# Measured durations in a generator that orders a decoder step for five engines

## The chip, the cores and the metric

The kernel runs on one core of a Trainium2 chip. The metric is the device time of one execution in microseconds (us); lower is better. Five engines each work through a list of instructions of their own, in order: TensorE (PE), VectorE (DVE), ScalarE (ACT), GpSimd (POOL) and SyncE (SP), which issues nearly all transfers. They wait for each other through semaphores only.

## The reference

One layer of a decoder, for 512 prompt tokens and for 8 sequences of 4 new tokens, each of which has 4096 tokens of past in a paged cache. In short:

```python
glu_a, glu_b, q, k, v, g_conv, g_att = split(x @ w_in)          # d_model 1024
u = glu_a * sigmoid(glu_b)
conv_out = silu(layer_norm(causal_depthwise_conv(u))) @ w_conv_proj
z = q @ k_all.T / 8 + sb_bias                                    # 8 heads of 64, keys: past pages + new
log_1m = log_sigmoid(-z) where the mask allows, else 0
a = exp(log_sigmoid(z) + cumsum_from_the_right(log_1m) - log_1m) # stick-breaking attention
att_out = (a @ v_all) @ w_att_proj
mixed = (sigmoid(g_conv) * conv_out + sigmoid(g_att) * att_out) @ w_out
x = layer_norm(alpha * x + mixed)
y = layer_norm(alpha * x + swiglu(x) + sigmoid(x @ w_ple_gate) * (p @ w_ple))
```

Everything is float32. The cache holds 8 x 32 pages of keys and as many of values that this step reads, 512 pages of 256 KB each, 134 MB in all.

## The kernel before, in words

**Products.** The prompt and the 32 new tokens stand side by side as 544 columns. A product of the main line (tile `g`) multiplies 128 x 128 of a weight with 272 columns (256 or 288 in some stages, 512 for q, k and the attention projection). Weights and activations are split in a high and a low half (`wh`, `wl`; `xh`, `xl`), and each product is made in three passes (`passes`). A weight comes in units of 512 KB: a raw tile (`wr`, three buffers, or `wq` and `wa` in the big pool), which ACT or DVE copies to `wh` and DVE or POOL subtracts from to get `wl`. A raw tile is free again when its second `wl` is done.

**Decode attention.** 32 chunks, each of 2 pages of keys for 4 sequences (8 transfers, `kv<-in_ck`) and the 8 pages of values (`kv<-in_cvv`). A page is one transfer. For each chunk PE makes scores (`z<-kv,qblk`, 16 matmuls, 32 records in the trace), ACT and DVE make the attention weights (`dz`, `dl`, `dp`, a scan that carries `cnew` from chunk to chunk), PE transposes them (`tp<-cct,dz`) and multiplies them with the values (`av<-kv,dp`, 8 matmuls, 16 records). Page tiles come from a pool of 39 slots that other tiles use too; at most 17 hold pages at a time (a tile is two pages), fewer in some stages.

**Prompt attention and convolution.** Prompt attention (`pa_pair`: `z<-qk`, `tp<-qk`, tiles `pa` and `pb`) and the convolution on DVE (`c<-u,cvt,c`, 120 instructions of 128 x 512) run beside the first third of the main line.

**Stages of the main line.** x times w_in (`g<-xh`), attention projection (`g<-ohl`), convolution projection (`g<-sh`), w_out (`g<-m`, in two halves of the columns A and B), the first feed-forward units and the embeddings (`g<-x1h`, `g<-ph`), the rest of the feed-forward part (`g<-x1h` with 272 columns, `g<-h`) and the last norm. After the last chunk the new tokens' attention output passes through w_att_proj and w_out by twelve weight tiles (`wa`; products `z<-wa,o_s` and `z<-wa,m_s`) and a norm of its own (`sq_s`, `r_s`, `y_s`), and only then can the 272-column feed-forward products start.

**What sets the order.** The program is written by a generator at build time. `Weave` keeps a clock for PE (`t`), ACT, DVE, POOL and the transfers (`dma`), all in us of an imagined execution. Each stream of work (main line, page loads, scores, decode, prompt attention, convolution, norms) is a Python generator that yields until a tile is ready by these clocks, and the scheduler lets the first stream go on that may. `mm` and `tr` add an estimate to PE's clock, `Engine` one to the clock of ACT, DVE or POOL, `moved` one to that of the transfers. `tt` and `split` choose between DVE, POOL and ACT by which is estimated to end first. So the numbers set no time on the chip; they set in which order each engine's instructions stand, and on which engine some of them run. On the chip each list is worked through in that order, and an instruction that must wait holds up all that is behind it on its engine. This is as true of SP: `prefetch` (pages) and `loader` (weights) write into one list.

Of the kernel before, what the change touches and what calls it, by code (L numbers as in the profile page):

```python
# [56 lines left out]
class Weave:  # L57
# [10 lines left out]
    def op(self, clock, us, out, reads):  # L68

        start = max([getattr(self, clock), self.t] + [self.ready.get(a.name, 0.0) for a in reads])  # L70
        setattr(self, clock, start + us)
        self.ready[out.name] = max(self.ready.get(out.name, 0.0), start + us + LAT)

# [54 lines left out]
class Engine:  # L128
# [6 lines left out]
    def __getattr__(self, name):  # L135
        fn = getattr(self.eng, name)

        def call(**kw):
            fn(**kw)  # L139
            out = kw["out"]  # L140
            reads = [v for k, v in kw.items() if k != "out" and hasattr(v, "space")]
            n = 1
            for d in out.shape[1:]:
                n *= d
            psum = any(a.space == PSUM for a in reads + [out])
            if self.clock == "act":
                ptr = sum(hasattr(kw.get(k), "space") for k in ("scale", "bias"))
                us = (n + (61 if psum else 112) + 56 * ptr) / 1200.0
                f = kw["func"]
                if f in (AF.Exp, AF.Ln, AF.Sigmoid) and self.table != (f == AF.Sigmoid):  # L150
                    self.table = f == AF.Sigmoid
                    us += 1.3
                reads = reads[:len(reads) - ptr]
            elif self.clock == "pool":
                us = (2 * n + 100) / 960.0
            else:
                ptr = sum(hasattr(kw.get(k), "space") for k in ("scalar", "scalar1", "scalar2", "initial"))
                if name in ("tensor_scalar", "tensor_copy") and not psum:
                    n = n / 2
                us = (n + 66 + 58 * ptr) / 960.0  # L160
            self.wv.op(self.clock, us, out, reads)
            for a in reads:
                if a.space == PSUM:
                    self.wv.read[a.name] = getattr(self.wv, self.clock) + LAT
        return call
# [3 lines left out]
def step_kernel(ctx: ExitStack, tc: tile.TileContext, xT, pT, ck, cvv, state, pt, W, cv, cc, yT, kT, vT, cvo):  # L169
    nc = tc.nc  # L170
    wv = Weave()
# [42 lines left out]
    def moved(ap):  # L214
        n = 4
        for d in ap.shape:
            n *= d
        wv.dma = max(wv.dma, wv.t + 1.5) + n / 0.357e6

    def load(eng, out, in_):  # L220
        eng.dma_start(out=out, in_=in_)  # L221
# [7 lines left out]

    def mm(us, out, lhsT, rhs, start, stop):  # L230
        T.matmul(out, lhsT=lhsT, rhs=rhs, start=start, stop=stop)  # L231
        wv.t = max(wv.t, wv.ready.get(lhsT.name, 0.0), wv.ready.get(rhs.name, 0.0), wv.free.get(out.name, 0.0)) + us
        wv.ready[out.name] = wv.t + 0.2

    def tr(out, in_):
        T.transpose(out, in_, ident)  # L236
        wv.t = max(wv.t, wv.ready.get(in_.name, 0.0), wv.free.get(out.name, 0.0)) + 0.11
        wv.ready[out.name] = wv.t + 0.2

# [79 lines left out]
    anew = con.tile([128, 2, 128], F32, name="anew")  # L319
# [3 lines left out]


    raw, hl, hs_, kept = {}, {}, {}, {}
    cur = {"t": 0, "pos": 0, "next": 0, "raw": 0, "w": 0, "kv": 0}

    def held(u):

# [68 lines left out]
    def passes(p, cols, k, nk, w, x):  # L398

        wh, wl = w  # L400
        xh, xl = x
        for a, b, st, sp in ((wh, xh, k == 0, False), (wh, xl, False, False), (wl, xh, False, k == nk - 1)):
            for s, c0, c1 in cols:
                mm((c1 - c0) * 4.25e-4, p[:, s, :c1 - c0], a, b[:, c0:c1], st, sp)

    def products(p, cols, nk, rhs, base, last=True):
        for k in range(nk):
# [101 lines left out]
    qk = []  # L509
    v_sb = {}  # L510
# [41 lines left out]
    def scores():  # L552
        for c in range(NCH):
            r = c // 16
            yield lambda: (c, 0, 3) in kv_t and c - n_scan[0] < 2
            ks_ = [kv_t.pop((c, 0, j)) for j in range(4)]
            yield on(*ks_)
            yield KMARGIN
            yield wv.bank("z")
            z = bank("z")  # L560
            for m in range(4):
                for j in range(4):
                    mm(0.127, z[32 * j:32 * j + 32, :256].rearrange("p (g c) -> p g c", g=2),
                       qblk[:, 4 * r + j, m, :], ks_[j][:, :, m * 128:(m + 1) * 128], m == 0, m == 3)
            del ks_
            cur["kv"] -= 4
            zb, l = d_tiles()
            S.activation(out=zb, in_=z[:, :256], func=AF.Identity, bias=cvt[:, SBR:SBR + 1])
            chain1(zb, l)
            z_t[c] = (zb, l)  # L570
            del zb, l

    def decode():
        yield on(qblk, ks)
        for r in range(2):
            yield wv.bank("z")
            z = bank("z")
# [23 lines left out]
        for r in range(2):  # L601
            carry = cnew[:, r:r + 1]
            yield wv.bank("av")
            av = bank("av")
            for n in range(16):
                c = 16 * r + n
                yield lambda: c in z_t
                zb, l = z_t.pop(c)
                yield on(l)
                p = d_sum()  # L610
                relu(p, zb)
                scan(p, l, carry)
                minus(zb, l)
                V.tensor_copy(out=carry, in_=l[:, 0:1])
                n_scan[0] += 1
                yield on(zb)
                chain3(zb)
                yield on(zb)
                yield DMARGIN
                yield wv.bank("tp")  # L620
                tp = bank("tp")
                for g in range(2):
                    tr(tp[:, g * 128:(g + 1) * 128], zb[:, g * 128:(g + 1) * 128])
                at = p
                S.activation(out=at, in_=tp[:, :256], func=AF.Copy)
                yield on(at)
                yield DMARGIN
                yield lambda: (c, 1, 3) in kv_t
                kvs = [kv_t.pop((c, 1, j)) for j in range(4)]
                yield on(*kvs)  # L630
                for g in range(2):
                    for j in range(4):
                        mm(0.235, av[32 * j:32 * j + 32, :], at[:, g * 128 + 32 * j:g * 128 + 32 * j + 32],
                           kvs[j][:, g, :], n == 0 and g == 0, False)
                del kvs, zb, l, at, p
                cur["kv"] -= 4
                yield
            yield lambda: ("vs", r) in v_sb
            for j in range(4):
                mm(0.235, av[32 * j:32 * j + 32, :], anew[:, r, 32 * j:32 * j + 32], v_sb["vs", r], False, True)  # L640
            yield spare(1)
            ob = tmp("ob")[:, :512]
            S.activation(out=ob, in_=av, func=AF.Copy)
            yield on(ob)
            yield wv.bank("tp")
            tp = bank("tp")
            for m in range(4):
                mm(0.11, tp[:, m * 32:m * 32 + 32], ob[:, m * 128:(m + 1) * 128],
                   cct[:, SEL + m * 32:SEL + m * 32 + 32], True, True)
            drop()  # L650
            for hh in range(2):
                V.tensor_copy(out=o_s[64 * hh:64 * hh + 64, :, r, :],
                              in_=tp[64 * hh:64 * hh + 64, :128].rearrange("p (m f c) -> p m f c", m=4, f=2)[:, :, hh, :])
# [3 lines left out]
    pa = {"live": 0, "next": 0}  # L657

    def pa_pair(idx, m, tiles):
# [5 lines left out]
        seg, n = [], 0  # L665
        for i in tiles:
            w = 128 * (i + 1)
            for z, r in zip(zs, rows):
                mm(w * 1.7e-3, z[:, n:n + w], qk[m][r, 0, 128 * i:128 * i + 128], qk[m][r, 1, :w], True, True)
            seg.append((i, n, w))  # L670
            n += w
        ab = []
        yield spare(2)
        for hh, z in enumerate(zs):
            h = 2 * m + hh
            a, b = slot("pa", (128, 2, 512)), tmp("pb")
# [38 lines left out]
        for i, c, w in seg:  # L715
            for kt in range(i + 1):
                for r, (zb, l) in zip(rows, ab):
                    mm(0.125, pa["o"][r, 128 * i:128 * i + 128], v_sb[m][:, kt * 128 + r.start:kt * 128 + r.stop],
                       l[:, c + kt * 128:c + (kt + 1) * 128], kt == 0, kt == i)
        if tiles[0] == 3:  # L720
            t = slot("ohl", (128, 2, 512), dt=F32R)
# [22 lines left out]
    us, cp = {}, []  # L744
# [77 lines left out]
    def project(nk, lhs, wt, out):  # L822
        yield wv.bank("z")
        z = bank("z")
        for h in range(2):
            yield on(*[wt(4 * h + j, 0) for j in range(4)])
            for k in range(nk):
                for j in range(4):
                    mm(0.075, z[32 * j:32 * j + 32, h * 128:(h + 1) * 128], lhs(k), wt(4 * h + j, k),
                       k == 0, k == nk - 1)  # L830
                if k % 2:
                    yield
# [599 lines left out]


LAT = 0.15
VBIAS = 2.0
GBIAS = 0.3
DMA_AHEAD = 5.0
# [107 lines left out]
```

## Time and profile before

| | us |
|---|---|
| median of 3 runs (1024.55 to 1028.53) | 1025.02 |
| the profiled execution | 1026.71 |
| its span, from first to last instruction | 1024.9 |
| PE busy / DVE / ACT / POOL | 977.8 / 636.1 / 484.3 / 166.5 |
| mean granted clock of PE | 0.986 |

The profile gives, for each engine, what it did and what ended its idle time. "Busy" of PE counts the time in which at least one matmul record is open. A wait is put down to what ended it. In the tables by stage a row is: start:end, length, busy us and count of PE, PE's weight loads (PEld), DVE, ACT and POOL, then the granted clock of PE, the mean busy share of the 16 transfer engines, and the GB/s that were moved. All times in the text are of the profiled execution, counted from the start of its span; it took 1.7 us longer than the median.

### The profile page before, as it was taken

What the parts mean: (1) busy time and instruction counts of PE and PEld (TensorE: products, weight loads), DVE (VectorE), ACT (ScalarE), POOL (GpSimd) and SP (SyncE); (2) the same over time, 40 slices, a digit from 0 to 9 for tenths busy, and PEclk for the clock granted to TensorE, in tenths of its full rate; (3) what the DMA queues carried; (4) which work ended last, traced back from release to release, by engine and by line L of the source; (5) the groups of instructions that cost most, each with busy time, mean ns of one, the idle gap of its engine ahead of it and who ended that gap; (6) DMA issues with size and microseconds to landing.
All of it is one profiled execution on the core that took longest, in us unless ns stands there. A gap on an engine that the chain in (4) does not pass through costs nothing.

```text
span 1024.9 us, 22484 instructions
## 1 busy us (share of the span) xinstructions
PE 977.8 (95%) x8242; PEld 856.9 (84%) x8242; DVE 636.1 (62%) x1005; ACT 484.3 (47%) x941; POOL 166.5 (16%) x156
## 2 busy tenths in 40 slices
PE   7989999899899999999999899999999999999994
PEld 6866676677777886788777899999999999999993
DVE  4798999999756456674976654333433345323376
ACT  4635666567785974343665543233332333222224
POOL 1320423223111002233322200000000012000021
PEclk9999999999999999999999999999999999999997
DMA  9949999999889999999989352222222222222302
GB/s 355 337 161 328 326 298 353 336 311 319 283 305 315 321 345 328 360 349 327 313 295 376 105 164 82 87 99 83 84 90 96 82 83 88 98 83 82 124 1 88
DMA packets 101376, 222.00 MB, mean 217 GB/s; under 512 B 11154, under 2 KB 14483, under 8 KB 101267
## 3 DMA queue, kind: packets, MB, share of 16 engines
q1 hardware_dynamic: 99394, 217.46, 61.4%
q10 hardware_dynamic: 1872, 3.11, 0.8%
q8 instruction: 65, 1.06, 0.4%
q14 instruction: 45, 0.36, 0.1%
HBM read 215.45 MB, written 5.07 MB: 215 GB/s over the span
## 4 chain that ended last, share of the span: by engine, by line
PE 76%; DVE 10%; DMA 7%; issue 2%; SPq 2%; ACT 2%; ACTq 0%; POOL 0%; DVEq 0%; POOLq 0%
PE g L231 63%; PE z L231 6%; PE av L231 5%; DVE c L139 3%; DMA kv<-in_ck 3%; PE tp L236 1%; DMA kv<-in_cvv 1%; SPq L221 1%; PE o L231 1%; DVE pb L139 1%; DMA wr<-in_W 1%; DVE wl L139 1%; DMA wa<-in_W 1%; SPq L536 1%; DVE dl L139 1%
## 5 line engine op out<-in xcount | busy, mean ns | idle before, releaser
L139 ACT ACTIVATE wh<-wr 128x512 fp32r<-128x512 f32 x236 | 146.5, 627 | 296.3 <-PE g L231 251.4
L139 DVE TENSOR_TENSOR wl<-wr,wh 128x512 fp32r<-128x512 f32 x193 | 134.0, 700 | 167.8 <-ACT wh L139 167.0
L231 PE MATMUL g<-x1h,wh 128*128 128x272 f32 (+2 forms) x832 | 183.7, 289 | 2.2 <-ACT x1h L139 1.5
L231 PE MATMUL g<-x1h,wl 128*128 128x272 f32 (+2 forms) x832 | 182.5, 288 | 0.0
L231 PE MATMUL g<-x1l,wh 128*128 128x272 f32 (+2 forms) x832 | 182.1, 288 | 0.0
L139 POOL TENSOR_TENSOR wl<-wr,wh 128x512 fp32r<-128x512 f32 x47 | 68.4, 1458 | 535.2 <-ACT wh L139 487.9
L231 PEld LDWEIGHTS g<-x1h,wh 128*128 128x128 f32 x832 | 134.9, 188 | 4.6 <-ACT x1h L139 1.7
L231 PEld LDWEIGHTS g<-x1l,wh 128*128 128x128 f32 x832 | 134.8, 189 | 0.0
L231 PEld LDWEIGHTS g<-x1h,wl 128*128 128x128 f32 x832 | 134.0, 189 | 0.0
L231 PE MATMUL g<-xh,wh 128*128 128x272 f32 (+1 forms) x512 | 128.1, 322 | 6.0 <-ACT wh L139 6.0
L231 PE MATMUL g<-h,wh 128*128 128x272 f32 x704 | 122.3, 290 | 0.0
L231 PE MATMUL g<-xh,wl 128*128 128x272 f32 (+1 forms) x512 | 119.8, 305 | 0.2 <-POOL wl L139 0.2
L231 PE MATMUL g<-xl,wh 128*128 128x272 f32 (+1 forms) x512 | 119.8, 305 | 0.0
L139 DVE SCALAR_TENSOR_TENSOR c<-u,cvt,c 128x512 f32<-128x512 f32 x120 | 113.3, 944 | 3.3
L231 PEld LDWEIGHTS g<-xh,wh 128*128 128x128 f32 x512 | 83.7, 192 | 26.4 <-issue 16.6
L231 PEld LDWEIGHTS g<-h,wh 128*128 128x128 f32 x704 | 103.1, 189 | 0.3
L231 PEld LDWEIGHTS g<-xh,wl 128*128 128x128 f32 x512 | 83.4, 191 | 3.9 <-POOL wl L139 0.8
L231 PEld LDWEIGHTS g<-xl,wh 128*128 128x128 f32 x512 | 84.0, 192 | 2.7 <-DVE xl L139 0.5
L231 PE MATMUL g<-h,wl 128*128 128x272 f32 x352 | 80.1, 289 | 0.0
L231 PE MATMUL z<-kv,qblk 128*32 128x256 f32 x1024 | 66.2, 382 | 1.9 <-DMA kv<-in_ck 1.9
L231 PE MATMUL av<-kv,dp 128*32 128x512 f32 x512 | 63.9, 612 | 0.0
L139 ACT ACTIVATE pa<-pa 128x384 f32<-128x384 f32 (+1 forms) x96 | 52.5, 555 | 17.4 <-DVE pa L139 15.7
(222 smaller groups left out, 1401.0 us busy)
## 6 DMA issues: line engine op xcount, KB each, us to landing
kv<-in_ck SPq DMA_DIRECT2D x256, 256.0 KB, 4.2
kv<-in_cvv SPq DMA_DIRECT2D x256, 256.0 KB, 5.3
wr<-in_W SPq DMA_DIRECT2D x120, 512.0 KB, 3.6
wq<-in_W SPq DMA_DIRECT2D x15, 512.0 KB, 6.0
wa<-in_W SPq DMA_DIRECT2D x12, 512.0 KB, 9.9
xr<-in_xT SPq DMA_DIRECT2D x8, 272.0 KB, 5.6
out_yT<-pw SPq DMA_DIRECT2D x7, 272.0 KB, 2.3
out_kT<-qk ACTq DMA_DIRECT2D x4, 272.0 KB, 5.2
```

Source lines behind the costliest of these rows:

```text
L139: fn(**kw)
L221: eng.dma_start(out=out, in_=in_)
L231: T.matmul(out, lhsT=lhsT, rhs=rhs, start=start, stop=stop)
L236: T.transpose(out, in_, ident)
L536: reg[col] = nc.sync.value_load(ptt[0:1, col:col + 1], min_val=0, max_val=POOL - 1)
```

## The change

Estimates are replaced, and three rules are added to the generator's clocks. A DVE and a POOL instruction that overlap lengthen each other (`SHARE`). A scan on DVE costs twice its length. PE pays 0.12 us (`TURN`) whenever the shape of the stationary operand changes. Transfers of one page go at 0.345 MB/us and others at 0.39 (both 0.357 before). The matmuls get other prices: the main line's 272 columns 0.125 us (0.116 before), scores 0.116 (0.127), the products of prompt attention half or less of what they had. No instruction is computed differently, and the number of matmuls, transfers and ACT instructions stays the same.

```diff
+        if clock == "dve":
+            us += min(SHARE * us, SHARE / (1 + SHARE) * max(0.0, self.pool - start))
+        elif clock == "pool" and self.dve > start:
+            both = min(us, self.dve - start)
+            us += 0.2 * both
+            self.dve += SHARE / (1 + SHARE) * both
...
+                elif name == "tensor_tensor_scan":
+                    n = 2 * n
...
-        wv.dma = max(wv.dma, wv.t + 1.5) + n / 0.357e6
+        wv.dma = max(wv.dma, wv.t + 1.5) + n / (0.345e6 if n == 262144 else 0.39e6)
...
+        turn(lhsT.shape)
...
-                mm((c1 - c0) * 4.25e-4, p[:, s, :c1 - c0], a, b[:, c0:c1], st, sp)
+                mm((c1 - c0) * 4.42e-4 + 0.005, p[:, s, :c1 - c0], a, b[:, c0:c1], st, sp)
...
-                    mm(0.127, z[32 * j:32 * j + 32, :256].rearrange("p (g c) -> p g c", g=2),
+                    mm(0.116, z[32 * j:32 * j + 32, :256].rearrange("p (g c) -> p g c", g=2),
...
-                mm(w * 1.7e-3, z[:, n:n + w], qk[m][r, 0, 128 * i:128 * i + 128], qk[m][r, 1, :w], True, True)
+                mm(w * 0.85e-3, z[:, n:n + w], qk[m][r, 0, 128 * i:128 * i + 128], qk[m][r, 1, :w], True, True)
...
-                    mm(0.125, pa["o"][r, 128 * i:128 * i + 128], v_sb[m][:, kt * 128 + r.start:kt * 128 + r.stop],
+                    mm(0.054, pa["o"][r, 128 * i:128 * i + 128], v_sb[m][:, kt * 128 + r.start:kt * 128 + r.stop],
...
+SHARE = 0.75
+TURN = 0.12
```

What this does to the lists shows at three places. (Helpers record the instructions, so all rows of an engine have one line number; it is 139 before and 146 now for DVE, 221 and 230 for SP, 231 and 240 for PE.)

**Ahead of the first scores, DVE.** The decode stream first attends to the new tokens' own keys, for two groups of sequences; `anew` and `cnew` of the second group must be done before the first page is used. Before, eight instructions of the convolution (`c`) stand in the midst of that group's steps:

```order
L139 SCALAR_TENSOR_TENSOR dz<-z,cvt,cct 128x16
L139 TENSOR_SCALAR c<-u,cvt 128x512
L139 SCALAR_TENSOR_TENSOR c<-u,cvt,c 128x512 x5
L139 TENSOR_SCALAR dp<-dz 128x16
L139 SCALAR_TENSOR_TENSOR dp<-dp,dl 128x16
L139 TENSOR_TENSOR dz<-dz,dp 128x16
L139 SCALAR_TENSOR_TENSOR c<-u,cvt,c 128x512 x2
L139 TENSOR_SCALAR pb<-pa 128x384
L139 SCALAR_TENSOR_TENSOR pb<-pb,pa 128x384
L139 TENSOR_TENSOR pa<-pa,pb 128x384
L139 COPY cnew<-dp 128x1
L139 COPY anew<-dz 128x16
```

Now the group's steps come before the first `u`, and the convolution begins behind them:

```order
L146 TENSOR_TENSOR dz<-dz,dp 128x16
L146 TENSOR_SCALAR pb<-pa 128x384
L146 SCALAR_TENSOR_TENSOR pb<-pb,pa 128x384
L146 TENSOR_TENSOR pa<-pa,pb 128x384
L146 COPY cnew<-dp 128x1
L146 COPY anew<-dz 128x16
L146 TENSOR_TENSOR wl<-wq,wh 128x512 x3
L146 TENSOR_TENSOR u<-g,sg 128x272
L146 TENSOR_TENSOR u<-g,sg 128x240
L146 TENSOR_TENSOR u<-g,sg 128x8x4
L146 TENSOR_SCALAR c<-u,cvt 128x512
L146 SCALAR_TENSOR_TENSOR c<-u,cvt,c 128x512
```

On PE the first scores have moved with that: ahead of them stand 192 matmuls of the main line now, 246 before; 48 of the 54 between have 512 columns.

**The end of the page loads, SP.** The list ends, before, with the last two pages, the twelve tiles of the new tokens' tail and 77 weight units. Seven more units stand between the last 25 pages, and `p`, the embeddings' input, somewhat ahead of them:

```order
L221 ISA
L221 DMA kv<-in_cvv 128x512
L221 DMA wa<-in_W 128x1024 x9
L221 DMA wr<-in_W 128x1024
L221 DMA wa<-in_W 128x1024 x3
L221 DMA wr<-in_W 128x1024 x76
```

Now no weight stands between the last 25 pages; `p` comes among the tail's tiles, and 84 units follow:

```order
L230 ISA
L230 DMA kv<-in_cvv 128x512
L230 DMA wa<-in_W 128x1024 x9
L230 DMA p<-in_pT 128x1088
L230 DMA wa<-in_W 128x1024 x3
L230 DMA wr<-in_W 128x1024 x84
```

**The last chunk, PE.** The last product with values stands, before, among the embeddings (`ph`), late in the stage that comes after w_out:

```order
L231 MATMUL g<-ph,wl 128x272 x2
L231 MATMUL av<-kv,dp 32x512 x8
L231 MATMUL av<-vs,anew 32x512 x4
L231 MATMUL g<-ph,wh 128x272 x2
L231 MATMUL g<-pl,wh 128x272 x2
```

Now it stands in the second half of w_out (`m`):

```order
L240 MATMUL g<-m,wl 128x256
L240 MATMUL av<-kv,dp 32x512 x8
L240 MATMUL av<-vs,anew 32x512 x4
L240 MATMUL g<-m,wh 128x256 x2
L240 MATMUL g<-m,wl 128x256
```

So 303 matmuls of the main line that stood ahead of it follow it: 129 of `m`, 96 of `x1h` with 256 columns, 78 of `ph`, and three of the norms. Between the first and the last chunk, all chunks have moved towards the front by much the same amount up to chunk 20, and by more and more after it. On the elementwise side 15 subtractions `wl` go from DVE to POOL (224 to 209 on DVE, 60 to 75 on POOL), and one `sl`, two `gc` and some of the norms' move too.

More of the change, by code (lines that the diff above doesn't have):

```diff
@@ L231, in mm, with turn @@
         T.matmul(out, lhsT=lhsT, rhs=rhs, start=start, stop=stop)
+        turn(lhsT.shape)
         wv.t = max(wv.t, wv.ready.get(lhsT.name, 0.0), wv.ready.get(rhs.name, 0.0), wv.free.get(out.name, 0.0)) + us
         wv.ready[out.name] = wv.t + 0.2
+    def turn(shape):
+        kind = shape[0], shape[1]
+        if cur["kind"] != kind:
+            cur["kind"] = kind
+            wv.t += TURN
     def tr(out, in_):
         T.transpose(out, in_, ident)
+        turn((128, 128))
         wv.t = max(wv.t, wv.ready.get(in_.name, 0.0), wv.free.get(out.name, 0.0)) + 0.11
@@ L325, in step_kernel @@
     raw, hl, hs_, kept = {}, {}, {}, {}
-    cur = {"t": 0, "pos": 0, "next": 0, "raw": 0, "w": 0, "kv": 0}
+    cur = {"t": 0, "pos": 0, "next": 0, "raw": 0, "w": 0, "kv": 0, "kind": None}
     def held(u):
@@ L632, in decode @@
                     for j in range(4):
-                        mm(0.235, av[32 * j:32 * j + 32, :], at[:, g * 128 + 32 * j:g * 128 + 32 * j + 32],
+                        mm(0.231, av[32 * j:32 * j + 32, :], at[:, g * 128 + 32 * j:g * 128 + 32 * j + 32],
                            kvs[j][:, g, :], n == 0 and g == 0, False)
@@ L639, in decode @@
             for j in range(4):
-                mm(0.235, av[32 * j:32 * j + 32, :], anew[:, r, 32 * j:32 * j + 32], v_sb["vs", r], False, True)
+                mm(0.231, av[32 * j:32 * j + 32, :], anew[:, r, 32 * j:32 * j + 32], v_sb["vs", r], False, True)
             yield spare(1)
@@ L828, in project @@
                 for j in range(4):
-                    mm(0.075, z[32 * j:32 * j + 32, h * 128:(h + 1) * 128], lhs(k), wt(4 * h + j, k),
+                    mm(0.058, z[32 * j:32 * j + 32, h * 128:(h + 1) * 128], lhs(k), wt(4 * h + j, k),
                        k == 0, k == nk - 1)
```

## The prediction

> **What bounds the kernel now.** First the page's head, its chain, and the table by stage.
>
> ```profile
> span 1024.9 us, 22484 instructions
> PE 76%; DVE 10%; DMA 7%; issue 2%; SPq 2%; ACT 2%; ACTq 0%; POOL 0%; DVEq 0%; POOLq 0%
> ```
>
> ```profile
> 0.00:52.00 52.00, 45.34 (x424) 38.15 (x425) 30.35 (x60) 28.72 (x57) 13.37 (x21) 1.00 0.96 347
> 52.00:68.00 16.00, 11.57 (x75) 8.55 (x74) 15.55 (x22) 4.15 (x8) 5.14 (x4) 0.89 0.29 106
> 82.00:200.00 118.00, 110.16 (x904) 79.71 (x903) 108.92 (x175) 73.15 (x151) 35.18 (x32) 0.99 0.95 327
> 200.00:300.00 100.00, 96.11 (x868) 74.58 (x867) 84.69 (x138) 72.26 (x146) 21.49 (x19) 0.97 0.90 302
> 400.00:515.00 115.00, 112.63 (x964) 88.84 (x964) 75.62 (x125) 49.49 (x102) 32.40 (x30) 0.99 0.96 335
> 538.00:560.00 22.00, 19.75 (x178) 15.92 (x180) 16.29 (x32) 13.43 (x31) 6.83 (x8) 0.92 1.02 401
> 590.00:1009.00 419.00, 419.00 (x3322) 418.55 (x3320) 181.17 (x259) 127.47 (x213) 20.16 (x14) 1.00 0.27 89
> 1009.00:1025.00 16.00, 1.36 (x6) 0.59 (x4) 9.72 (x13) 4.83 (x10) 4.91 (x3) 0.66 0.27 94
> ```
>
> From 590 to 1009 us PE never idles, and the matmuls are the same after the change: 419 us that stay. The tail of 16 us keeps its steps. All that can move lies ahead of 590 us, where PE is nearly full and the transfers are as well: their engines are busy 90 to 96% of 82 to 515. The exception is 52 to 68, with 0.29 and 106 GB/s.
>
> Next, what SP waited for, by stage, and how fast it issues pages:
>
> ```profile
> SPq L221 <- PE z L231: 13.9, 1, 13.9
> ...
> SPq L221 <- POOL wl L139: 4.1, 4, 1.5
> SPq L221 <- DVE wl L139: 3.2, 2, 1.9
> ...
> SPq L221 <- POOL wl L139: 4.1, 1, 4.1
> SPq L221 <- DVE sg L139: 1.7, 1, 1.7
> SPq L221 <- DVE wl L139: 0.9, 1, 0.9
> ```
>
> ```profile
> 408.79 8.29 SPq L221 DMA_DIRECT2D kv<-in_ck  x8
> ...
> 494.13 4.33 SPq L221 DMA_DIRECT2D kv<-in_cvv  x8
> ...
> 535.15 2.89 SPq L221 DMA_DIRECT2D kv<-in_cvv  x5
> 538.32 7.32 SPq L221 DMA_DIRECT2D wa<-in_W  x9
> ```
>
> The first row is the wait of 60 to 82 us, the next two those of 200 to 300, the last three those of 515 to 538; between them SP waits for no computing engine for more than 0.7 us at a time. Eight pages of keys take SP 8.3 us to issue, eight of values 4.3. So a chunk costs SP 12.6 us and its weights on top, and from 82 to 515 us the page stream, SP's list with the transfers behind it, goes at its own pace: nobody holds it up, and PE meets the pages soon after they land. This stream sets when the decode part ends. Only its one hole, where SP stands 13.9 us in front of a slot that the first scores had yet to free, is an order's doing.
>
> **The frame of the sum.** PE's work is fixed, so the end comes when the last value product (`av` of chunk 31) can run, plus the work that stands behind it.
>
> ```profile
> 488.08 6.66 PE g L231 x54
> ...
> 553.68 2.71 PE av L231 x24
> ...
> 589.64 386.61 PE g L231 x3066
> ```
>
> In this trace it starts at 553.6 us (the chain counts it from 553.68), and 1024.9 - 553.6 = 471.3 us follow. After the change 303 more matmuls follow: 225 of 256 columns at 6.66 / 54 = 0.123 us, 78 of 272 at 386.61 / 3066 = 0.126, and three of a norm at some 0.4 (estimated from the mean of 0.41 that the trace gives `o<-tot` ones, which is a latency): 27.7 + 9.8 + 1.2 = 38.7 us. If the last chunk came 38.7 us sooner, nothing would be won or lost.
>
> **Part 1, the start.** The convolution no longer stands ahead of the steps that the first scores need, and 48 matmuls of 512 columns and 6 others are gone from ahead of them.
>
> ```profile
> 44.44 4.82 DVE L139 SCALAR_TENSOR_TENSOR c<-u,cvt,c 128x512 f32<-128x512 f32 x5
> ...
> 49.77 3.51 DVE L139 SCALAR_TENSOR_TENSOR c<-u,cvt,c 128x512 f32<-128x512 f32 x2
> ...
> 58.75 0.69 PE L236 MATMUL tp<-cct,vt 128*128 128x128 f32 x2 [4.43 <-DVE v L139]
> ...
> 65.57 1.93 PE L231 MATMUL z<-kv,qblk 128*32 128x256 f32 x32
> ```
>
> The DVE steps win 8.3 us. On PE the 54 matmuls are some 12 us (0.23 for 512 columns, scaled from 0.126 for 272), and the 4.4 us wait for the copy of `v` now stands behind the first scores. So these start near 49 instead of 65.6. SP waited 13.9 us until they had read their tile, at 67.5: it came there at about 53.7, and now finds the slot free. The gain to the stream is the whole 13.9 us; at worst nothing, if the group's steps stay late.
>
> **Part 2, the stream's end.** Seven weight units and `p` leave the part ahead of the last page. At SP each costs the 0.43 of an issue, on the transfer engines 512 KB at 401 GB/s = 1.3 us: 3.5 to 10.5 us together. I take 6, nearer to the issue, since it is SP that is full. With them go the waits of 515 to 538, 4.1 + 1.7 + 0.9 = 6.7 us. Of the 7.3 us of such waits in 200 to 300 I strike half, 3.6: the stream is earlier there, yet more `wl` are POOL's. So the last page is issued at 538.0 - 13.9 - 6 - 6.7 - 3.6 = 507.8, and lands 5.3 us later (the page's median for values, last row below) at 513.1.
>
> ```profile
> L231 PE MATMUL z<-kv,qblk 128*32 128x256 f32 x1024 | 66.2, 382 | 1.9 <-DMA kv<-in_ck 1.9
> ...
> kv<-in_ck SPq DMA_DIRECT2D x256, 256.0 KB, 4.2
> kv<-in_cvv SPq DMA_DIRECT2D x256, 256.0 KB, 5.3
> ```
>
> **Part 3, from there to PE.** The last keys land about 5 us before the last values; then come 1.9 us of scores, 57 matmuls of `m` (7.0), and two transposes (0.4): the last `av` at some 517.5, 36.1 us earlier than now, 2.6 short of the 38.7. The estimate's order wants the pages sooner than the stream has them, so PE will wait for keys in the last ten chunks, 0.3 to 0.7 us at a time, where before it waited for ACT and DVE. That is why the many PE waits of the first half bring nothing: what is saved there is waited out at the pages.
>
> ```profile
> PE tp L236 <- ACT pa L139: 7.2, 5, 2.5
> PE tp L236 <- DVE v L139: 6.3, 3, 4.4
> ...
> PE g L231 <- DVE wl L139: 2.3, 1, 2.3
> ...
> PE g L231 <- ACT x1h L139: 1.5, 1, 1.5
> PE av L231 <- DVE sq_s L139: 1.2, 2, 0.9
> ```
>
> The last two stand behind the last chunk (the new tokens' norm). They go, 2.7 us, since 129 matmuls of `m` now stand there as cover. Next late are the tail's tiles: twelve `wa` and `p` at 1.3 us take until 513.1 + 17 = 530; PE is at the second half of `z<-wa,m_s` some 13 us after `av`, at 530.5. No wait, but no room either: with the stream later by a microsecond, the end is later by one.
>
> **Part 4, DVE to POOL.** 15 `wl` move.
>
> ```profile
> L139 DVE TENSOR_TENSOR wl<-wr,wh 128x512 fp32r<-128x512 f32 x193 | 134.0, 700 | 167.8 <-ACT wh L139 167.0
> L139 POOL TENSOR_TENSOR wl<-wr,wh 128x512 fp32r<-128x512 f32 x47 | 68.4, 1458 | 535.2 <-ACT wh L139 487.9
> ```
>
> DVE is rid of 15 x 0.70 = 10.5 us and POOL has 21.9 more. Neither is what ends a stage while the stream does; I cost it at nothing, under cover of the pages. Without that cover it is between -10.5 and +11.4 (every POOL instruction in the way of DVE). The Trainium skill, "SBUF — State Buffer", section "Who interferes with whom", says that the port pair which VectorE and GpSimd share is an exclusive lock; by that the sum would be the +11.4. This trace shows contention, if not how much: the convolution's instruction takes 4.82 / 5 = 0.96 us at 44 us.
>
> **The sum.** 1024.9 + 2.6 - 2.7 = 1024.8 us of span, 1.8 around it, so 1026.6 profiled, against 1026.71. That is 1.7 above the median as now; against 1025.0 it says 1024.9. The unsure terms lean to a gain (the whole price of the moved units, 4.5 more; SP's waits of 200 to 300, 3.7 more), so I say 1023.5.
>
> **Rivals.**
> *The stream is not at its pace (faster).* In 538 to 560 the engines move 401 GB/s, in 200 to 300 only 302. If SP, with fewer weights to wait for, gains 10 us more over 450, PE sets the pace; then count what it waited for ahead of the last chunk, 7.2 + 6.3 + 2.3, and its clock, 16 x (1 - 0.89) + 100 x (1 - 0.97) = 4.8 us: 20.6 in all. Two thirds of it gives 1011. For it: the generator's other prices also fit this trace now. Against it: SP's rows, 12.6 us a chunk without a wait.
>
> *POOL holds the raw tiles (slower).* A `wl` on POOL frees its raw tile 0.76 us later, and takes its turn in a longer queue; SP's list has the next unit in front of pages. Before, four such waits cost 4.1 us in 200 to 300. If each of the 15 costs 0.8 us, the stream ends 12 us later and the time is 1036. It decides from 5 us on. The shared lock would do the same by way of DVE, 92% busy in 82 to 200.
>
> *The hole stays (slower).* If the first scores are still late, 13.9 us come back: 1038.
>
> *Half clock.* The granted clock falls in 52 to 68, 200 to 300 and 538 to 560. The Trainium skill, "TensorE: Matmul & The Clock Gate", section "What's actually happening", puts the fall after an idle window of about 3.4 us; by that only the 4.43 us wait would cost, and the new waits for pages nothing. The trace has the fall in 200 to 300 too, where the longest wait for ACT is 2.5 us: the trace decides, and a page wait above 2 us costs up to 1.7 more. It is in the upper end of the range.
>
> **Numbers.** No change within 0.5%, which is about what a measurement can tell here (1019.9 to 1030.1): 0.42. The faster rival, 0.33. Slower 0.25: POOL's tiles 0.17, the hole 0.08. The range reaches from below the faster rival to the slower one, 1009 to 1037; for the likeliest case alone it is 1018 to 1029.
>
> **What would show it.** Right: the wait of SP for `z` near 67 us is gone; the first scores near 49; PE waits for `kv<-in_ck` in many chunks after the twentieth, more than the 1.9 us of now; the last `av` near 517; PE full from some 555. Wrong: the last `av` before 512 or after 522; SP's waits for `wl` above 15 us ahead of the last page; transfers above 350 GB/s from 82 to 515; a first score after 55.

## The result, and the profile after

| | before | after |
|---|---|---|
| median, us | 1024.78 (4 runs, 1023.27 to 1028.53) | 1042.78 (4 runs, 1040.69 to 1043.81) |
| ratio | | 1.0168, 95% interval 1.0136 to 1.0199 |
| span of the profiled run, us | 1024.9 | 1038.9 |

The change makes the kernel slower by 1.7%, which is outside the range of the forecast. First the head of the page after, its chain, and the stages as they were shown of before (start:end, length, busy us and count of PE, PEld, DVE, ACT and POOL, granted clock, transfer share, GB/s):

```profile
span 1038.9 us, 22488 instructions
PE 980.7 (94%) x8242; PEld 856.5 (82%) x8242; DVE 641.8 (62%) x983; ACT 486.9 (47%) x941; POOL 199.7 (19%) x178
PE 71%; DVE 10%; DMA 7%; SPq 4%; issue 3%; ACT 2%; POOL 1%; ACTq 0%; DVEq 0%; POOLq 0%
...
52.00:68.00 16.00, 14.80 (x127) 9.74 (x119) 14.82 (x23) 7.34 (x18) 2.70 (x2) 1.00 0.98 338
...
82.00:200.00 118.00, 110.72 (x907) 76.21 (x905) 104.33 (x165) 72.70 (x152) 34.25 (x35) 0.99 0.94 322
200.00:300.00 100.00, 94.31 (x863) 74.10 (x863) 90.73 (x131) 66.98 (x135) 40.02 (x31) 0.98 0.93 315
...
538.00:560.00 22.00, 17.58 (x141) 16.82 (x139) 21.45 (x41) 12.96 (x31) 11.75 (x9) 1.00 0.14 49
```

The hole is closed: 52 to 68 us moves 338 GB/s, 106 before. What is new stands at 538 to 560: transfers at 49 GB/s, 401 before, and DVE busy for 21.45 of 22 us. The stream of pages is over by then, and PE waits all the same. Two rows of before, and the same two of after, put the loss into place:

```profile
0.00:490.00 490.00, 465.69 (x4029) 360.72 (x4030) 368.64 (x591) 291.34 (x586) 115.45 (x114) 0.99 0.92 319
490.00:600.00 110.00, 101.72 (x966) 87.02 (x965) 82.86 (x155) 65.68 (x144) 25.98 (x25) 0.97 0.74 260
```

```profile
0.00:490.00 490.00, 462.26 (x3999) 349.03 (x4000) 365.69 (x570) 294.85 (x592) 132.66 (x126) 0.99 0.95 330
490.00:600.00 110.00, 93.99 (x895) 84.65 (x894) 82.81 (x143) 56.90 (x122) 38.10 (x33) 0.97 0.54 192
```

PE's idle time grew from 24.3 to 27.7 us ahead of 490, and from 8.3 to 16.0 in 490 to 600: 3.4 and 7.7. PE's busy time grew by 2.9 (980.7 against 977.8) with as many matmul records, 8242; what lengthened them no run here shows. That makes 14.0, the whole difference of the spans. The medians differ by 18.0: the profiled execution of the changed kernel is the fastest of its four, and that of the kernel before is 1.9 above its median, so some 4 us of the loss lie outside these two traces. Where the 7.7 lie, the waits of PE in 490 to 600 say (us in total, times, longest), after:

```profile
PE g L240 <- DVE sg L146: 4.7, 2, 3.0
PE g L240 <- ACT dz L146: 4.6, 1, 4.6
PE o L240 <- POOL tot L146: 2.7, 1, 2.7
PE g L240 <- DVE wl L146: 1.7, 1, 1.7
PE z L240 <- DMA kv<-in_ck: 1.1, 2, 0.7
PE g L240 <- DVE rr L146: 0.8, 1, 0.8
```

The chain through the 4.6 us wait (start, length, engine and what it did):

```profile
505.33 2.39 PE z L240 x32
...
509.14 0.42 ACT dl L146
509.56 0.28 ACT ln L146
...
509.86 4.11 DVE rr L146 x3
513.97 1.29 DVE dp L146
...
515.28 1.64 DVE dl L146
...
517.41 0.43 ACT dz L146
...
517.91 1.62 PE g L240 x6
...
521.63 2.71 PE av L240 x24
```

And the rows of DVE and PE where the wait ends:

```profile
517.35 0.42 DVE L146 TENSOR_TENSOR rr<-g,rr 128x256 f32<-128x256 f32 x1
...
517.91 0.77 PE L240 MATMUL g<-m,wh 128*128 128x256 f32 x2 [4.55 <-ACT dz L146]
```

The scores of the last chunk end at 507.7, in time. Then their steps on DVE (`dp`, the scan `dl`) stand behind three instructions of the main line's first norm (`rr`), which take 4.11 us. PE stops for 4.55. The instruction that waits is a product of the main line, which does not read `dz`. DVE's `rr<-g,rr`, which reads an earlier product out, ends at 517.77, and `dz` on ACT at 517.83; which of the two let PE go, the trace cannot tell. Both stand behind the same steps of DVE.

The second place comes after w_out. The last product of w_out before, and after, and the steps of DVE that end the two norms (`x1l`, 8 instructions for each half of the columns; count, shortest, median and longest in ns, first and last start); of after, also PE's waits at that place:

```profile
522.63 0.28 PE L231 MATMUL g<-m,wl 128*128 128x256 f32 x1
...
L139 DVE SCALAR_TENSOR_TENSOR x1l<-rr,cvt,x1h x16: 472/475/1486, 508.3 to 554.0; 128x256 fp32r<-128x256 f32 x16
```

```profile
549.51 0.28 PE L240 MATMUL g<-m,wl 128*128 128x256 f32 x1
...
L146 DVE SCALAR_TENSOR_TENSOR x1l<-rr,cvt,x1h x16: 471/474/960, 534.2 to 584.4; 128x256 fp32r<-128x256 f32 x16
...
553.23 0.70 PE L240 MATMUL o<-tot,on_m 128*128 128x256 f32 x2 [2.72 <-POOL tot L146]
564.09 0.52 PE L240 MATMUL g<-ph,wh 128*128 128x272 f32 x2 [1.70 <-DVE sg L146]
579.49 0.82 PE L240 MATMUL g<-ph,wh 128*128 128x272 f32 x2 [3.03 <-DVE sg L146]
```

From the end of the last product of w_out to the end of the last `x1l` go 31.5 us before and 35.1 after: the second norm, a chain on DVE, ACT and POOL, ahead of the 272-column products. Before, PE had in that time 94 products of `x1h` and 78 of `ph` (21 us) and the decode of a whole chunk, scores and values. After, it had 94 and 91, and no chunk: all decode work was done.

### The profile page after: what moved, and what is told of

It is laid out like the page before. It is cut to its first block, busy times and chain, and to the rows that moved or that the text cites. A ratio compares the mean times of both kernels' runs of the same rounds, so it can differ in the third digit from the quotient of the medians.

```text
span 1038.9 us, 22488 instructions
## 1 busy us (share of the span) xinstructions
PE 980.7 (94%) x8242; PEld 856.5 (82%) x8242; DVE 641.8 (62%) x983; ACT 486.9 (47%) x941; POOL 199.7 (19%) x178
## 4 chain that ended last, share of the span: by engine, by line
PE 71%; DVE 10%; DMA 7%; SPq 4%; issue 3%; ACT 2%; POOL 1%; ACTq 0%; DVEq 0%; POOLq 0%
PE g L240 59%; PE z L240 5%; PE av L240 5%; DMA kv<-in_ck 3%; SPq L230 3%; DMA kv<-in_cvv 3%; DVE rr L146 3%; DVE c L146 2%; SPq L554 2%; PE tp L253 1%; PE o L240 1%; DVE wl L146 1%; POOL wl L146 1%; DVE pw L146 1%; DVE ln L146 1%
## 5 line engine op out<-in xcount | busy, mean ns | idle before, releaser
L146 DVE TENSOR_TENSOR wl<-wr,wh 128x512 fp32r<-128x512 f32 x181 | 129.4, 720 | 185.1 <-ACT wh L146 184.6
L146 POOL TENSOR_TENSOR wl<-wr,wh 128x512 fp32r<-128x512 f32 x59 | 87.0, 1475 | 586.7 <-ACT wh L146 558.4
L146 DVE SCALAR_TENSOR_TENSOR c<-u,cvt,c 128x512 f32<-128x512 f32 x120 | 110.0, 916 | 3.3
L240 PEld LDWEIGHTS g<-xh,wh 128*128 128x128 f32 x512 | 82.4, 190 | 33.1 <-issue 23.3
L240 PE MATMUL z<-kv,qblk 128*32 128x256 f32 x1024 | 68.3, 388 | 3.7 <-DMA kv<-in_ck 3.1
L240 PEld LDWEIGHTS z<-kv,qblk 128*32 128x32 f32 x1024 | 35.2, 111 | 30.7 <-issue 9.8
```

## Experiments

In all edits the main line's products and their order stay as they are. "Place" means how many us of matmuls, estimated from the rows' durations, stand ahead of a point in PE's program; the last `av` stands 26.2 us behind the end of w_out before, 24.9 ahead of it after. Ratios are against runs of the kernel before on the same chip (medians 1024.5 to 1027.2).

| run | us | ratio, 95% interval |
|---|---|---|
| hold_last_two | 1030.31 | 1.0048, 1.0029 to 1.0067 |
| no_pool_at_norms | 1033.86 | 1.0072, 1.0052 to 1.0092 |
| hold_and_no_pool | 1026.12 | 1.0015, 0.9994 to 1.0037 |
| hold_no_pool_wide | 1024.09 | 0.9992, 0.9974 to 1.0011 |
| before_no_pool | 1018.99 | 0.9944, 0.9919 to 0.9969 |
| before_no_pool_wide | 1018.97 | 0.9943, 0.9922 to 0.9964 |
| places_from_20 | 1028.34 | 1.0031, 1.0013 to 1.0048 |
| places_from_4 | 1027.21 | 1.0017, 1.0001 to 1.0032 |
| places_no_pool | 1030.17 | 1.0038, 1.0022 to 1.0054 |
| no_turn | 1024.82 | 0.9982, 0.9958 to 1.0006 |
| no_turn_no_pool | 1020.78 | 0.9959, 0.9943 to 0.9974 |
| no_share | 1039.31 | 1.0135, 1.0117 to 1.0153 |
| share_070 | 1037.33 | 1.0113, 1.0092 to 1.0134 |
| dma_alone | 1029.81 | 1.0045, 1.0024 to 1.0066 |
| turn_alone | 1056.79 | 1.0275, 1.0234 to 1.0317 |
| turn_alone_hold | 1046.10 | 1.0207, 1.0166 to 1.0247 |
| turn_places_20 | 1042.18 | 1.0155, 1.0121 to 1.0188 |
| turn_places_4 | 1043.81 | 1.0157, 1.0131 to 1.0183 |

**The last two chunks held behind w_out.**

```diff
-            yield lambda: (c, 0, 3) in kv_t and c - n_scan[0] < 2
+            yield lambda: (c, 0, 3) in kv_t and c - n_scan[0] < 2 and (c < 30 or 'woB' in flag)
```

> The changed kernel, with one edit: the scores of the last two chunks may not be ordered before the last product of w_out (m). Up to chunk 29 every list is that of the changed kernel; the last av then stands 19.7 us of matmuls behind the end of w_out (24.9 ahead of it in the changed kernel, 26.2 behind it in the one before). Theory COVER: the loss is that the decode products that lay beside the two norms after w_out have been used up earlier; it expects the waits of PE in 505 to 590 us (14.9 us in the changed kernel, 8 in the one before) to fall to about 6, and with half a clock window or two less the time to come down 8 to 16 us, to 1026 to 1035. Theory CROWD: the loss comes from instructions that went from DVE to POOL and slow each other down at the norms; it expects no change beyond 4 us: 1039 to 1046. Theory SCATTER (any reordering moves the time by so much): no forecast, anything from 1015 to 1050.

12.5 us came back. PE's idle time in 490 to 600 fell from 16.0 to 7.3 us (110 less the 102.66 of the row), though the last `av` runs at 554 instead of 521.6:

```profile
490.00:600.00 110.00, 102.66 (x995) 95.03 (x995) 87.15 (x157) 63.26 (x134) 35.14 (x32) 1.00 0.63 217
```

The norms got no shorter by it: from the end of the last product of w_out to the end of the last `x1l` go 38.1 us here. PE had work in that time. So the early end of the last two chunks, which the forecast took for the goal, was most of the loss. The edit moves their work on PE and their steps on DVE together; how much of the 12.5 is the one and how much the other, it does not say.

**Nothing shared out to POOL at the norms.**

```diff
-        e = G if end("pool", (2 * n + 100) / 960, in0, in1) + GBIAS < ...
+        e = G if not ('m' in flag and ("x1", 1, 3) not in flag) and end("pool", ...
```

> The changed kernel, with one edit: from the start of w_out until the second norm is done, whatever may go to DVE or POOL goes to DVE (12 subtractions wl, 2 rr, 2 ln, 2 h). The order on PE is the same to within 0.7 us of matmuls. CROWD: the doubled DVE instructions there (rr 1.78 instead of 0.68, sg 1.50 instead of 0.42) go, and with them most of the loss: 1027 to 1034. COVER: DVE has about as much to do as before, since what overlapped is now in line; the waits for sg, tot and dz stay within 3 us: 1039 to 1046.

8.9 us came back, as CROWD had it; COVER, which the first edit bore out, had forecast no change. The order on PE is nearly that of the changed kernel, and its idle time in 490 to 600 fell from 16.0 to 8.9 us:

```profile
490.00:600.00 110.00, 101.14 (x964) 91.47 (x964) 81.84 (x170) 62.95 (x134) 11.51 (x15) 1.00 0.60 206
```

The rows of DVE at the place of the 4.55 us wait, first the changed kernel, then this one:

```profile
509.86 4.11 DVE L146 TENSOR_TENSOR rr<-rr,ln 128x512 f32<-128x512 f32 x3 [4.79 <-ACT ln L146]
513.90 1.35 DVE L146 TENSOR_SCALAR dp<-dz 128x256 f32<-128x256 f32 x1
515.28 1.63 DVE L146 TENSOR_TENSOR_SCAN dl<-dl,cnew,dp 128x256 f32<-128x256 f32 x1
```

```profile
509.25 2.50 DVE L146 TENSOR_TENSOR rr<-rr,ln 128x512 f32<-128x512 f32 x4 [5.09 <-ACT ln L146]
511.66 0.29 DVE L146 TENSOR_SCALAR dp<-dz 128x256 f32<-128x256 f32 x1
511.99 0.75 DVE L146 TENSOR_TENSOR_SCAN dl<-dl,cnew,dp 128x256 f32<-128x256 f32 x1
```

Four `rr` in 2.50 us where three took 4.11 beside POOL, which did the fourth and a `wl` meanwhile. PE's wait at this place falls from 4.55 to 1.0 us (that of the transposes for `dz`). Handing a quarter of the `rr` to POOL, with a `wl` behind it, made the chain longer. The Trainium skill, "SBUF — State Buffer", section "Who interferes with whom", calls the port pair that VectorE and GpSimd share an exclusive lock; the trace agrees in direction. The forecast had cited that rule and costed the part at nothing.

**Both edits, and the second on the kernel before.**

> The changed kernel with both edits: the last two chunks held behind w_out, and nothing shared out to POOL from the start of w_out to the end of the second norm. The one gave 12.5 us, the other 8.9. ONE LOSS (both edits take away the same waits of PE at the norms, one by matmuls that cover them, one by a shorter chain on DVE): 1026 to 1032, little under the better of the two. TWO LOSSES: the gains add, 1018 to 1024.

> The kernel before, with nothing shared out to POOL from the start of w_out to the end of the second norm (10 subtractions wl fewer on POOL). If overlap with POOL costs only where the norms have no cover, which the kernel before has (last av 24.0 us behind the end of w_out): 1022 to 1029, no change. If it costs wherever it happens, it gives here what it gave in the changed kernel: 1014 to 1019.

Both together give 16.7, not 21.4: mostly one loss, reached from two sides. But the kernel before gains 5.5 from the POOL edit by itself, and is then, with the wide form below, the fastest of all that were run: 0.6% ahead of the kernel before, some 2% ahead of the changed one. So the overlap cost before the change too. The 3.4 between the 8.9 and the 5.5 is less than the intervals can tell: that the change added to this cost is not shown.

```profile
490.00:600.00 110.00, 105.57 (x1031) 93.54 (x1030) 85.24 (x174) 68.11 (x148) 12.46 (x14) 1.00 0.77 268
```

That is the kernel before with the edit, in the fastest of its executions: 4.4 us idle instead of 8.3, and a granted clock of 1.00 instead of 0.97. The same edit with `'pa' in flag` for `'m' in flag`, from some 200 us on:

> The changed kernel with the last two chunks held behind w_out, and nothing shared out to POOL from the end of the prompt attention (some 200 us) instead of from w_out, to the end of the second norm (51 subtractions on POOL; 64 with the narrow edit, which took 1026.1). WIDE (overlap costs in 200 to 400 us too, where POOL now overlaps DVE for 59 us, 39 before): 1018 to 1023. NORMS ONLY (the pages set the pace there, so it is hidden): 1024 to 1029.

> The kernel before, with nothing shared out to POOL from the end of the prompt attention to the end of the second norm (42 subtractions on POOL; 50 with the narrow edit, which took 1019.0). WIDE: 1013 to 1017. NORMS ONLY: 1017 to 1022.

Against the narrow edit, neither differs by more than the intervals can tell: between 200 us and w_out no cost of the overlap shows.

**All chunks back at their old places.** `PLACE[c]` holds the number of main-line matmuls ahead of chunk c in the kernel before; chunks 0 to 3 stay early.

```diff
+                cur["g"] += 1
                 mm((c1 - c0) * 4.42e-4 + 0.005, p[:, s, :c1 - c0], a, b[:, c0:c1], st, sp)
...
-            yield lambda: (c, 0, 3) in kv_t and c - n_scan[0] < 2
+            yield lambda: (c, 0, 3) in kv_t and c - n_scan[0] < 2 and cur["g"] >= PLACE[c]
```

> The changed kernel with one edit: from chunk 4 on, the scores of a chunk may not be ordered before as many matmuls of the main line have been as in the kernel before (last av 21.1 us behind the end of w_out). Chunks 0 to 3 stay early, so the hole of SP stays closed; 68 subtractions on POOL (60 before, 75 in the changed kernel). PLACES (the whole loss is where the chunks stand): 1021 to 1028, as the kernel before. PLACES AND HOLE (the closed hole is a gain that the places had eaten): 1010 to 1018. NOT ONLY PLACES (the other moves of the change cost too): 1029 to 1036.

> As the first, but from chunk 20 on; chunks 0 to 19 stand where the changed kernel has them. If only the last two chunks cost: as with these two held, 1028 to 1033. If the last twelve do: 1021 to 1028, as the first of this call. If the first twenty cost by waits for pages: 2 to 6 us above the first of this call.

> The same with nothing shared out to POOL from the start of w_out to the end of the second norm (58 subtractions on POOL). To be set against 1019.0 for the kernel before with that edit, and 1026.1 for the changed kernel with the last two chunks held and that edit. PLACES: 1016 to 1022. NOT ONLY PLACES: 1023 to 1028. With the closed hole as a gain: 1007 to 1014.

1027.2 and 1028.3: with the places the loss goes, but for 0.2% and 0.3%. Where the first twenty chunks stand makes no difference that can be told. The last two alone gave 1030.3, and its interval overlaps that of places_from_20: what the other ten of the last twelve add is not shown. The closed hole shows no gain either: with the scores at 48.7 and the old places behind them, the stream soon stands still elsewhere, which the row of places_from_4 shows (273 GB/s, 327 before in the same stretch):

```profile
82.00:200.00 118.00, 106.50 (x825) 77.30 (x824) 104.62 (x162) 72.74 (x148) 38.49 (x36) 0.94 0.82 273
```

The third missed every band: here the POOL edit gained nothing, and reads 3 us worse. Both kernels have a stall of their own, since the edit holds the last scores but not the transposes behind them: 57 products of the main line stand between the two in the kernel before, 18 here. In places_from_4 it is

```profile
551.06 0.69 PE L253 MATMUL tp<-cct,dz 128*128 128x128 f32 x2 [6.54 <-ACT dz L146]
```

So 1027 need not be the best of that order. The 3 us are no more than what orders of like places differ by (next part), so what sharing out to POOL costs in this order stays open.

**Parts of the change.** `TURN = 0.0`, `SHARE = 0.0` and `SHARE = 0.70` in the changed kernel; the POOL edit (wide) on the first; and the kernel before with the transfer rates alone.

> The changed kernel with PE's 0.12 us for a change of shape set to 0. The first scores stay early (35.8 us of matmuls into the program), the last av stands 2.9 us behind the end of w_out, and 75 subtractions stay on POOL as in the changed kernel. COVER: the last av nearer to the place it had before, the page hole gone: 1018 to 1032. CROWD: as the changed kernel, 1038 to 1046.

> The changed kernel with PE's 0.12 us for a change of shape set to 0 (1024.8 us alone), and nothing shared out to POOL from the end of the prompt attention to the end of the second norm. If what the overlap cost in the other three (5.5, 8.9 and, with the hold, 4.2 us) is to be had here too: 1015 to 1021, faster than the kernel before. If it is hidden here, with PE waiting 12.7 us ahead of 490 us: 1022 to 1027.

> The changed kernel without the rule that DVE and POOL slow each other (SHARE 0). 60 subtractions stay on POOL, as before the change; first scores at 49.8 us of matmuls, as before; the last av stands 6.0 us ahead of the end of w_out. By places, between 2.9 us behind (1024.8) and 24.9 ahead (1042.8): 1027 to 1034. If the overlap of DVE and POOL that this rule moves were the loss: 1021 to 1026.

> The changed kernel with SHARE 0.70 instead of 0.75: a control for scatter. The last av stands 23.8 us of matmuls ahead of the end of w_out (24.9 in the changed kernel), 75 subtractions on POOL as there, but rows change places in many spots. If the place of the last chunks and what runs beside the norms set the time: 1039 to 1047, as the changed kernel. If any reordering moves the time at random by what the runs so far span: outside of that, with a chance of two in three.

> The kernel before, with the transfer rates of the change alone. It too closes the hole at 53.7 to 67.5 us (first scores 35.8 us of matmuls into the program, 49.0 before), and its last av stands 12.9 us earlier in PE's program than before, still 11.3 us behind the end of w_out. The prediction's frame (the page stream keeps its pace and ends about 14 us earlier, PE's program has moved forward by as much): 1020 to 1027. If the closed hole were a gain by itself: 1008 to 1016. If any step of the last av towards w_out costs as it does in the changed kernel (14 us for 51): 1027 to 1031.

Without TURN the last `av` stands 2.9 us behind w_out, and the loss is gone; with the POOL edit the kernel is 0.4% ahead of the one before, though this interval overlaps that of no_turn. The rates alone move the last `av` by 12.9 us, close the hole, and cost 5. The control came out 1.7 us below its band: neighbours with like places differ by some 5 us, as the expectation for scatter had it, so a difference of that size between two orders proves little here. This holds for the 5.5 of before_no_pool too. For it speaks that the POOL edit was faster in four orders of five, clear of the intervals in two of them, the kernel before and the changed one. The 12.5 of hold_last_two and the whole loss are well above such scatter. no_share missed by 5: its hole is open (first scores at 65.7 us), its chunks stand early all the same, and PE waits for keys

```profile
PE z L240 <- DMA kv<-in_ck: 10.7, 11, 2.2
```

where the changed kernel waits 3.1 us in all. Early chunks need an early stream.

**TURN alone.**

> The kernel before, with one part of the change alone: PE's estimated 0.12 us at each change of the stationary shape. It moves the decode furthest forward: first scores 35.8 us of matmuls into the program (49.0 before, 36.5 in the changed kernel), the last av 33.1 us ahead of the end of w_out. No subtraction goes to POOL for it (56 on POOL, 60 before, 75 in the changed kernel). COVER: as slow as the changed kernel or slower, 1040 to 1052. CROWD: as the kernel before or faster, 1010 to 1026.

> The kernel with PE's 0.12 us alone (1056.8 us), and the last two chunks held behind the end of w_out (last av 20.4 us behind it, 33.1 ahead without the edit). Chunks up to 29 stand even earlier than in the changed kernel (chunk 20 at 271 us of matmuls, 290 there, 305 before). COVER at the norms as the whole cause: 1026 to 1036. If the early chunks cost by themselves, by waits for pages all along (PE has 36 us of waits ahead of 500 us there, 29 in the changed kernel, 24 before): 1038 to 1050.

> The kernel with PE's 0.12 us alone (1056.8 us; 1046.1 with its last two chunks held), with chunks 20 to 31 held at the places of the kernel before, counted in matmuls of the main line. Chunks up to 19 stay further ahead than in any other kernel (chunk 10 at 143.3 us of matmuls, 166.2 before, 151.3 in the changed kernel). PLACES OF THE LAST TWELVE: 1026 to 1033, as the changed kernel with that edit (1028.3). If chunks as early as that cost by themselves: 1036 to 1044.

> The same with chunks 4 to 31 held at the places of the kernel before. PLACES: 1024 to 1031, as the changed kernel with that edit (1027.2). NOT ONLY PLACES (what else the 0.12 us reorder costs): 1033 to 1045.

The last `av` 33.1 us ahead of w_out gave 1056.8, above even COVER's band, and holding two chunks gave 10.7 back, much as in the changed kernel, though 1046 is 10 above the band of COVER as the whole cause. The places explain little more of it: 1042 with the last twelve back and 1044 with all but the first four. Of the other 16 us, some 8 lie ahead of 490 us (turn_places_4: 32.6 us idle, 24.3 before):

```profile
0.00:490.00 490.00, 457.45 (x3906) 350.56 (x3907) 364.68 (x586) 288.66 (x569) 104.86 (x110) 0.98 0.91 312
```

There PE waits in front of transposes, for `pa` 11.3 and for `v` 8.9 us (7.2 and 6.3 before). TURN without the other prices makes further moves that cost, and which of them, no run shows. In the changed kernel they do not show: its places put back give 1027.

## Why the prediction was wrong

Up to the landing of the last page its places in the trace came true almost to the digit; behind it they did not, nor did the sum:

| step | forecast | measured |
|---|---|---|
| SP's wait for `z` near 67 us | gone | gone |
| first scores | 49 | 48.2 |
| last page issued, landed | 507.8, 513.1 | 508.0, 513.0 |
| transfers, 82 to 515 us | below 350 GB/s | 315 to 337 |
| last `av` starts | 517.5 | 521.6 |
| from there to the end | 471.3 + 38.7 - 2.7 = 507.3 | 517.3 |
| PE idle behind it (18.6 before) | 2.7 less | 6.2 more |
| PE full from | 555 | 579.5 |

```profile
48.24 1.93 PE L240 MATMUL z<-kv,qblk 128*32 128x256 f32 x32
...
503.19 4.80 SPq L230 DMA_DIRECT2D kv<-in_cvv  x8
```

The differences add up: 1024.8 + 4.1 + 10.0 = 1038.9, the span of the profiled run.

**The step that failed is the frame of the sum**, "the end comes when the last value product can run, plus the work that stands behind it". It counts the 303 matmuls that moved behind the last `av` as 38.7 us of work without gaps, and takes 2.7 us of waits away. Measured are 1038.9 - 521.6 = 517.3 us behind it, 10.0 more than that. Nearly all of the 10.0 is idle time: PE idles 6.2 us more there than before, not 2.7 less. That the matmuls would add 38.7 us of work was right to some 1 us. The main line has an end of its own, the last product of w_out and then some 30 us of norm on DVE, ACT and POOL, and the decode of the last chunks was what PE did meanwhile. The frame held the stream for the only late one. hold_last_two shows it: 12.5 us for putting that work back.

**Part 3, the last 4.1 us of `av`.** 2.6 us were forecast as page waits. These are small (3.1 us in all, 1.9 before). What came instead is the 4.55 us wait at 513: the last chunk's steps on DVE now stand between those of the first norm. "They go, 2.7 us, since 129 matmuls of `m` now stand there as cover" was right for the waits that it looked at (`sq_s` 0.3 us now, `x1h` none), and blind to the new ones: this one, and those for `tot`, `wl` and `sg` behind w_out.

**Part 4, POOL, "I cost it at nothing, under cover of the pages".** In the second norm there are no pages left, and in the first PE waits for DVE all the same. The range that it gave for the case without cover, up to +11.4, holds the 8.9 that no_pool_at_norms measured, but by luck: that edit takes 12 `wl` and six other instructions off POOL at one place, not the 15 that moved, and a like edit gave 5.5 in the kernel before. The forecast said that the trace did not show how much DVE and POOL slow each other. It did: the convolution's instruction takes 0.75 us where POOL is idle, and 1.65 in the median where POOL works for at least half of its time (71 and 40 of the 120).

**Part 1 and 2** hold, and not only in their sum: SP is 14.2 us ahead of the kernel before at the 49th page (13.9 forecast for the hole), 19.3 at the 481st and 30.0 at the last (30.2 forecast). But the gain had no taker. In places_from_4, with the same early start, those 14.2 us are spent by the 145th page, and the time is that of the kernel before but for 0.2%.

**The rivals.** The faster one fell: transfers kept their 315 to 337 GB/s. POOL's raw tiles cost SP nothing more: it waited for `wl` 6.6 us in 82 to 515, 8.3 before. The slower one had a like price, 1036, at the wrong place; none told of the norms. The half clock was the same in number: five falls of 3.41 us ahead of the tail in both traces, behind waits of 1.5 to 4.4 us before and of 2.3 to 4.6 us after. So waits well below the 4.43 us cost a fall too, as the forecast took from the trace. That the time would be "no change" rested on the frame and on nothing for Part 4.

## What to carry to other kernels

When an order moves work of one stream ahead of another's, ask what that work covered where it stood. A stage whose end is a chain on slower engines needs filler, and truer estimates can spend the filler early. A sum of PE's work behind a point is a lower bound until every chain that ends behind that point is followed too. And sharing elementwise work out to a second engine is worth pricing at the place where it lies on the path: in this one, sharing nothing out there was faster in the kernel before and in the changed one, though not in every order between them.

## What the runs showed of the hardware

Beside a POOL instruction, DVE's can take two to nearly five times as long, those with one input and the scan included: `rr` 1.37 instead of 0.63 us each, `dp` 1.35 instead of 0.29, the scan 1.63 instead of 0.75, in the rows above. Not each one does: of the scans that overlap POOL for half of their time or more, some take 0.75 us in the changed kernel, and the longest 1.78. POOL's own lengthen by less: of the 59 `wl<-wr` on POOL in the changed kernel, the 12 beside which DVE is busy for less than 85% of the time take 1.34 us in the mean, the other 47 take 1.51. DVE alone does two `wl` in 1.28 us (at 513.5 in no_pool_at_norms). One on each engine at 531.5 in the changed kernel takes 1.96 from the first start to the last end. So here an overlapped pair gains nothing.
